# Stacked high and low parts for the last 64 rows of the feed-forward width in both down products

## The chip, the core and the metric

The kernel runs on one core of a Trainium2 chip. The metric is the device time of one execution in microseconds (us). The core has a matrix engine (TensorE; its weight loads have a row of their own in the profile, PEld), a vector engine (VectorE, DVE), a scalar engine (ScalarE, ACT), GpSimd (POOL), a queue that issues DMAs (SyncE, SP), and 16 DMA engines. The engines run side by side, each in its own order, and wait for each other through semaphores.

## The reference

One layer of an encoder on x of 1024 positions by 1024 channels, in float32, in three steps. The first and the last are feed-forwards of width 2752:

```python
def swiglu(x, w_gate, w_up, w_down):
    return (jax.nn.silu(x @ w_gate) * (x @ w_up)) @ w_down

h = layer_norm(ALPHA * h + 0.5 * swiglu(h, ffn1_w_gate, ffn1_w_up, ffn1_w_down), ln1_g, ln1_b)
h = layer_norm(ALPHA * h + hybrid_mixer(h, ...), ln2_g, ln2_b)
h = layer_norm(ALPHA * h + 0.5 * swiglu(h, ffn2_w_gate, ffn2_w_up, ffn2_w_down), ln3_g, ln3_b)
```

The mixer between them has one input projection, windowed attention with three strides, a Fourier branch, gates and an output projection. The change concerns the product with `w_down` in both feed-forwards, which contracts over the 2752 hidden channels.

## The kernel before

**Numbers.** A float32 operand is split into a high part (rounded to the format fp32r, in which TensorE takes float32 data in one pass) and a low part (what is left). A product is the sum of three matmuls, `TERMS` in line 331: high by high, high by low, low by high. `split` (line 340) makes the parts: `hi` copies on ScalarE (line 346), `lo` subtracts on VectorE (line 350); `pick` (line 337) chooses one.

**Products.** Each large product is a two by two block product done with seven block products instead of eight (`PROD`, line 380: product p multiplies one combination of the left blocks by one of the right blocks). The hidden width of 2752 is 21 blocks of 128 and a rest of 64. The blocks are taken in 11 pairs (`PAIRS`); a pair's even block belongs to the first half of the contraction and its odd block to the second. The odd block of the last pair, j = 10, is the rest of 64 rows, padded with zeros to 128: in `tail_after` (line 725) VectorE writes zeros to rows 64 to 127 of the hidden tile, and `_layouts` (line 2168) pads the weights with zero rows. The products that contract over odd blocks are 2 (a12 by b21), 3 (s4 by b22) and 4 (a22 by t4). Of their last pair, 64 rows of each operand or of one of them are zeros.

**The down product.** `ffn` (line 622) is called for tag "a" (the first feed-forward) and tag "b" (the second). Hidden tiles go to HBM (`spill`), and come back as steps: `load_step` (line 811) fetches, for product p and pair j, 512 columns of the left operand into the left half of a page and 512 columns of the right operand into the right half, two DMAs on SP's queue; `split` cuts the page into parts; `step` (line 819) issues 12 matmuls in line 827, three terms for each of four row tiles of 128, each 512 columns wide, into four PSUM banks. The order of the products is 1, 6, 2, 5, 3, 7, and in "a" then 4; their accumulators are X (products 1 and 2), Y (6), Z (5 and 3), V (7) and U (4). In "b" product 4 is done row tile by row tile: `load_b4` (line 856) keeps all right blocks in six pages (`qbb0` to `qbb5`), `load_a4` (line 863) fetches a strip of the left operand into two pages (`qab`, and `qsb` for pairs 8 to 10), and `last_steps` (line 844) issues 33 matmuls a row tile in line 852.

**The order of the work.** A planner, `Flow` (line 73), writes the program. TensorE's large jobs keep the order in which they are registered (`job`, with a cost in us: `MM` = 0.2267 a matmul); small ones are put between them when they are ready. Tasks of VectorE and ScalarE and loads are placed by the time at which the job that needs them is due, less a lead (34 us for the splits of the steps, 44 for their loads). The planner's clock goes by these costs alone; on the chip each engine then runs its list in order. So a change of a cost can shift the order of the lists.

**Names used below.** Tiles are named by their step: `qa210h` and `qa210l` are the parts of tag a, product 2, pair 10; `qb78l` is the low part of tag b, product 7, pair 8. Line 462 is the matmul of the gate, up and mixer input projections. Line 1600 is attention's product with the values, plain float32, which the trace shows as two records a matmul; where a window of keys is cut, it has pieces of 64 rows at rows 0 to 63 and 64 to 127. Line 1120 is a product of 32 rows by 387 columns, done once.

Of the kernel before, what the change touches and what calls it, by code (L numbers as in the profile page):

```python
# [10 lines left out]
F32 = mybir.dt.float32  # L11
F32R = mybir.dt.float32r
# [4 lines left out]
P = 128  # L17
# [2 lines left out]
KD = 8  # L20
FF = 2752
NFULL = FF // P
HEAD_DIM = 128
NH = 12
SLOTS = 4
# [16 lines left out]
PAIRS = 11  # L42
# [30 lines left out]
class Flow:  # L73
# [11 lines left out]
    def job(self, us, fn, banks=0, deps=(), **kw):  # L85
        self.jobs.append(Node("P", us, fn, deps, banks=banks, **kw))
        return self.jobs[-1]
# [82 lines left out]
    def short(self):  # L170

        return min((n.key for q in self.open.values() for n in q if not self.can(n) and self.shown(n)), default=1e9)
# [98 lines left out]
class Builder:  # L271
# [7 lines left out]
    def page(self, name, dt=F32):  # L279
        return self.sb.tile([P, 1024], dt, name=name, tag="pg", bufs=NPG)  # L280
# [15 lines left out]
def kernel(  # L296
# [6 lines left out]
    nc = tc.nc  # L303
    kb = Builder(ctx, tc)
    fl = Flow()
    page, half, bank = kb.page, kb.half, kb.bank
    V, S, G, Q, F, job = fl.V, fl.S, fl.G, fl.Q, fl.F, fl.job
    x, out = x[0], out[0]
# [22 lines left out]
    TERMS = (("hi", "hi"), ("hi", "lo"), ("lo", "hi"))  # L331
    MM = 0.2267
    stt = nc.vector.scalar_tensor_tensor
    L, R = slice(0, 512), slice(512, 1024)
    W, B, H, J = {}, {}, {}, {}

    def pick(parts, kind):
        return parts[0 if kind == "hi" else 1]

    def split(name, get, put, deps=(), need=None, lead=14.0, w=1024, pages=2, gives=1):  # L340

        st = {}

        def hi():
            st["h"] = page(name + "h", F32R)
            nc.scalar.activation(st["h"][:, :w], get()[:, :w], AF.Copy)

        def lo():
            t = page(name + "l", F32R)
            nc.vector.tensor_sub(t[:, :w], get()[:, :w], st["h"][:, :w].bitcast(F32))  # L350
            put((st["h"], t))
        us = 0.15 + w * 1.06e-3
        if isinstance(need, tuple):

            def piece(i):
                cs, last = slice(i * 512, (i + 1) * 512), None

                def hi_():
                    if i == 0:
                        st["h"] = page(name + "h", F32R)  # L360
                    nc.scalar.activation(st["h"][:, cs], get()[:, cs], AF.Copy)

                def lo_():
                    if i == 0:
                        st["l"] = page(name + "l", F32R)
                        put((st["h"], st["l"]))
                    nc.vector.tensor_sub(st["l"][:, cs], get()[:, cs], st["h"][:, cs].bitcast(F32))
                sn = S(0.6, hi_, deps[i], need[i], lead + 1.5, 1.3, pages=0 if i else 2)
                return V(0.69, lo_, [(sn, 0.1)], need[i], lead, gives=gives if i else 0)
            return [piece(0), piece(1)]  # L370
        s = S(0.15 + w * 0.88e-3, hi, deps, need, lead + 1.5, us + 0.6, pages=pages)
        return V(us, lo, [(s, 0.1)], need, lead, gives=gives)


# [97 lines left out]
    def put(c, names, parts):  # L472
        for i, n in enumerate(names):
            W[c, n] = tuple(t[:, i * 512:(i + 1) * 512] for t in parts)
# [147 lines left out]
    def ffn(tag, X, w_gu, w_tail, w_dn, load_rest, norm, rest_deps=None, sums_at=None, by_tile=False):  # L622

        HN = {}
        hs = {(n, j): kb.dram([P, 512], f"hs{tag}{n}{j}") for n in COMBOS for j in range(PAIRS)}
        PARTS = ((0, 4), (4, 8), (8, 11))
        TAIL = FF - NFULL * P
# [119 lines left out]
        c0 = ck[0]  # L747
        first = {"a11": J[c0, 1], "a12": J[c0, 2], "a21": None, "a22": J[c0, 4]}
# [14 lines left out]
        q = Q(J[tl, 0], 0.5, load_tail, pages=1)  # L763
# [20 lines left out]
        for si, (to, x0, x1) in enumerate(sums):  # L784
            for i in range(3):
# [7 lines left out]
                a = Q(at[0], 1.0, copy, [tdn[x0, i]] if x0 not in blk else [], lead=0.0)  # L793
# [3 lines left out]
        D_, Y, T, sm = {}, {}, {}, {}  # L797
# [4 lines left out]
        def source(n, j):  # L802
            if n in blk:
                return w_dn[blk[n], j]
            i = part_of(j)
            return td[n, i][j - PARTS[i][0]]

        def source_nodes(n, j):
            return [tdn[n, part_of(j)]] if n not in blk else []

        def load_step(p, j):
            def run():
                D_[p, j] = t = page(f"q{tag}{p}{j}")
                xn, wn = PROD[p]
                nc.sync.dma_start(t[:, L], hs[xn, j])
                nc.sync.dma_start(t[:, R], source(wn, j))
            return run

        def step(p, j, set_, first):
            def run():  # L820
                if first and j == 0:
                    for m in range(4):
                        B[tag, set_, m] = bank(f"{set_}{tag}{p}{m}")
                q = D_.pop((p, j))
                for m in range(4):
                    for ti, (a, b) in enumerate(TERMS):
                        nc.tensor.matmul(B[tag, set_, m], pick(q, a)[:, m * P:(m + 1) * P], pick(q, b)[:, R],  # L827
                                         start=first and j == 0 and ti == 0,
                                         stop=j == PAIRS - 1 and ti == 2, skip_group_check=True)
            return run  # L830

        if tag == "a":
# [3 lines left out]
        for p in (1, 6, 2, 5, 3, 7) if by_tile else (1, 6, 2, 5, 3, 7, 4):  # L836
            for j in range(PAIRS):
                first = p not in (2, 3)
                J[tag, "d", p, j] = n = job(12 * MM, step(p, j, SET[p], first), 4 if first and j == 0 else 0, gives=2)
                q = Q(n, 0.5, load_step(p, j), [(HN[PROD[p][0], j], 4.0)] + source_nodes(PROD[p][1], j), 44.0, pages=1)  # L840
                split(f"q{tag}{p}{j}", lambda p=p, j=j: D_[p, j], lambda t, p=p, j=j: D_.__setitem__((p, j), t), [q], n,
                      34.0)

        def last_steps(m, j0, j1):
            def run():
                if j0 == 0:
                    B[tag, "U", m] = bank(f"U{tag}{m}")
                for j in range(j0, j1):
                    aa, o = (D_["a", m], j) if j < 8 else (D_["as", m], j - 8)
                    bb, bs = D_["b", j // 2], slice((j % 2) * 512, (j % 2) * 512 + 512)  # L850
                    for ti, (a, b) in enumerate(TERMS):
                        nc.tensor.matmul(B[tag, "U", m], pick(aa, a)[:, o * P:(o + 1) * P], pick(bb, b)[:, bs],
                                         start=j == 0 and ti == 0, stop=j == PAIRS - 1 and ti == 2)
            return run

        def load_b4(i):
            def run():
                D_["b", i] = t = page(f"qb{tag}{i}")
                for j in range(2 * i, min(2 * i + 2, PAIRS)):
                    nc.sync.dma_start(t[:, (j % 2) * 512:(j % 2) * 512 + 512], source("t4", j))  # L860
            return run

        def load_a4(m):
            def run():
                D_["a", m], D_["as", m] = t, s = page(f"qa{tag}{m}"), page(f"qs{tag}{m}")
                for j in range(PAIRS):
                    dst = t[:, j * P:(j + 1) * P] if j < 8 else s[:, (j - 8) * P:(j - 7) * P]
                    nc.sync.dma_start(dst, hs["a22", j][:, m * P:(m + 1) * P])
            return run

        if by_tile:
            for m in range(4):
                for i, (j0, j1) in enumerate(PARTS):
                    J[tag, "u", m, i] = job(3 * (j1 - j0) * MM, last_steps(m, j0, j1), 1 if i == 0 else 0,
                                            gives=(4 if i == 2 else 0) + (12 if i == 2 and m == 3 else 0))

            for i in range((PAIRS + 1) // 2):
                n = J[tag, "u", 0, 0]
                deps = [x for j in range(2 * i, min(2 * i + 2, PAIRS)) for x in source_nodes("t4", j)]
                q = Q(n, 0.5, load_b4(i), deps, 88.0 - 8.0 * i, pages=1)  # L880
                split(f"qb{tag}{i}", lambda i=i: D_["b", i], lambda t, i=i: D_.__setitem__(("b", i), t), [q], n,
                      80.0 - 8.0 * i, 512 * min(2, PAIRS - 2 * i))
            for m in range(4):
                n = J[tag, "u", m, 0]
                q = Q(n, 0.75, load_a4(m), [(HN["a22", j], 4.0) for j in range(PAIRS)], pages=2)
                split(f"qa{tag}{m}", lambda m=m: D_["a", m], lambda t, m=m: D_.__setitem__(("a", m), t), [q], n)
                split(f"qs{tag}{m}", lambda m=m: D_["as", m], lambda t, m=m: D_.__setitem__(("as", m), t), [q], n, w=384)

        if rest_deps:
            rest_deps = rest_deps(ck)  # L890
# [334 lines left out]
    for p, bk, new in VORDER:  # L1225
        n = PROD[p][1]
        for i in range(2):
            value_part(n, i, (vblk if n in vblk else vt)[n][i], [vtn[n]] if n in vtn else (), VJ[p, 0], 14.0)
    for m in range(8):
        st = {}  # L1230
# [978 lines left out]
```

## Time and profile before

| | us |
|---|---|
| median of 3 runs | 2070.76 (2070.5 to 2072.65) |
| the profiled execution | 2072.24 |
| its span, first to last instruction | 2070.3 |
| TensorE matmul busy | 2058.5 (99%) |
| TensorE weight loads busy | 1713.6 (83%) |
| VectorE busy | 1276.4 (62%) |
| ScalarE busy | 910.4 (44%) |

The down products lie at 420 to 633 us (tag a) and 1853 to 2063 us (tag b) of the span. The page's busy times are of one profiled execution; matmuls are pipelined, so the start of a record tells more than its length, and the distance of two starts is the pace. In the rows, `128*128 128x512` is a matmul of 128 rows by 128 weight columns whose result is 128 by 512, and `64*128` one that contracts over 64 rows. SPq is SyncE's queue as it issues DMAs.

### The profile page before, as it was taken

How to read it: one execution, taken by the hardware profiler on the slowest of the kernel's cores; microseconds unless marked ns; L12 is line 12 of the kernel's file. 1: busy time of each engine (PE TensorE's matmuls, PEld its weight loads, DVE VectorE, ACT ScalarE, POOL GpSimd, SP SyncE). 2: the span in 40 equal slices, each digit the busy share in tenths (PEclk: the TensorE clock that was granted, in tenths of full speed). 3: DMA queues.
4: the chain of work that ended last, by engine and by line, in shares of the span. 5: the costliest groups of instructions: out<-in, count | busy, mean ns of one | idle time of the engine just before them, and what ended most of it. 6: DMA issues, size and time to landing. Idle time of an engine off the chain costs nothing.

```text
span 2070.3 us, 25541 instructions
## 1 busy us (share of the span) xinstructions
PE 2058.5 (99%) x9523; PEld 1713.6 (83%) x9523; DVE 1276.4 (62%) x1757; ACT 910.4 (44%) x1441; POOL 233.6 (11%) x404
## 2 busy tenths in 40 slices
PE   9999999999999999999999999999999999999998
PEld 7888888888888888888888888888888888888887
DVE  7865555576554658455556764763877665575565
ACT  6433333555475324455455443318633333355342
POOL 0122111010000010021121111000011101010000
PEclk9999999999999999999999999999999999999999
DMA  5778875599743336467786659523144433357743
GB/s 203 236 239 260 253 220 169 177 341 404 257 160 120 102 122 182 142 178 204 207 218 198 226 185 384 184 97 138 60 169 179 157 132 127 123 202 273 263 159 105
DMA packets 151292, 401.29 MB, mean 194 GB/s; under 512 B 18338, under 2 KB 40690, under 8 KB 150720
## 3 DMA queue, kind: packets, MB, share of 16 engines
q1 hardware_dynamic: 111648, 266.38, 37.2%
q0 software_dynamic: 39520, 133.28, 21.5%
q8 instruction: 74, 1.21, 0.2%
q14 instruction: 50, 0.41, 0.1%
HBM read 303.41 MB, written 153.84 MB: 221 GB/s over the span
## 4 chain that ended last, share of the span: by engine, by line
PE 97%; ACT 1%; DMA 1%; DVE 0%; issue 0%; DVEq 0%; SPq 0%
PE Ab L462 14%; PE Aa L462 13%; PE Aq L462 8%; PE Da L462 6%; PE Db L462 5%; PE As L462 5%; PE wo L2078 3%; PE Dq L462 3%; PE Zb L827 3%; PE Xb L827 3%; PE Za L827 3%; PE Xa L827 3%; PE pj L1991 2%; PE v L1238 2%; PE Ds L462 2%; PE pv L1600 2%
## 5 line engine op out<-in xcount | busy, mean ns | idle before, releaser
L1568 ACT ACTIVATE p<-p,stat 128x192 f32<-128x192 f32 (+2 forms) x96 | 42.3, 442 | 17.0 <-DVE stat L1563 16.0
L326 POOL DMA_DIRECT2D hsaa<-t2a x21 | 12.0, 571 | 317.1 <-DVE t2a L696 299.0
L1358 DVE SCALAR_TENSOR_TENSOR oq<-Dq,b_cols,t2q 128x512 f32<-128x512 f32 x12 | 11.8, 986 | 50.8 <-PE Dq L462 50.8
L326 POOL DMA_DIRECT2D hsba<-t2b x21 | 11.4, 543 | 279.6 <-DVE t2b L696 279.6
L1600 PEld LDWEIGHTS pv<-pT,v 128*128 128x128 f32 (+1 forms) x320 | 37.3, 189 | 6.1 <-ACT pT L1589 1.0
L692 DVE TENSOR_TENSOR t2b<-Db,t2b 128x512 f32<-128x512 f32 x21 | 14.5, 691 | 44.9 <-PE Db L462 44.9
L692 DVE TENSOR_TENSOR t2a<-Da,t2a 128x512 f32<-128x512 f32 x21 | 14.5, 691 | 44.4 <-PE Da L462 44.4
L600 ACT ACTIVATE t2a<-Aa 128x512 f32<-128x512 f32 x21 | 12.6, 600 | 65.5 <-PE Aa L462 65.4
L1600 PE MATMUL pv<-pT,v 128*128 128x128 f32 (+1 forms) x320 | 40.8, 289 | 0.5 <-ACT pT L1589 0.5
L600 ACT ACTIVATE t2b<-Ab 128x512 f32<-128x512 f32 x21 | 12.6, 599 | 62.9 <-PE Ab L462 62.9
L1553 DVE SCALAR_TENSOR_TENSOR p<-sc,bias 128x512 f32<-128x512 f32 (+1 forms) x40 | 24.7, 620 | 25.0 <-PE sc L1539 20.6
L326 POOL DMA_DIRECT2D n_spill<-y x16 | 8.6, 538 | 264.5 <-ACT y L1008 264.5
L1539 PE MATMUL sc<-oq,oq 128*128 128x192 f32 (+2 forms) x192 | 34.1, 322 | 0.0
L684 DVE TENSOR_TENSOR t3a<-Da,t3a 128x512 f32<-128x512 f32 x21 | 14.5, 690 | 27.8 <-PE Da L462 26.4
L1539 PEld LDWEIGHTS sc<-oq,oq 128*128 128x128 f32 x192 | 29.8, 190 | 2.0
L1358 DVE SCALAR_TENSOR_TENSOR oq<-Dq,b_cols,t3q 128x512 f32<-128x512 f32 x12 | 11.8, 987 | 30.1 <-PE Dq L462 30.1
L462 PE MATMUL Db<-Zs40h,usb 128*128 128x512 f32 x84 | 29.4, 391 | 0.7 <-DVE t3b L684 0.7
L462 PE MATMUL Db<-Zs41h,usb 128*128 128x512 f32 x84 | 29.3, 389 | 0.0
L462 PE MATMUL Da<-Xs40h,usa 128*128 128x512 f32 x84 | 29.3, 389 | 0.0
L462 PE MATMUL Da<-Xs41h,usa 128*128 128x512 f32 x84 | 29.3, 389 | 0.0
L684 DVE TENSOR_TENSOR t3b<-Db,t3b 128x512 f32<-128x512 f32 x21 | 14.5, 690 | 20.7 <-PE Db L462 16.0
L1563 DVE TENSOR_REDUCE stat<-p 128x2 f32<-128x384 f32 (+2 forms) x40 | 24.5, 620 | 1.2
(7340 smaller groups left out, 7210.4 us busy)
## 6 DMA issues: line engine op xcount, KB each, us to landing
qa<-hsas SPq DMA_DIRECT2D x44, 256.0 KB, 5.9
qa<-tdat SPq DMA_DIRECT2D x44, 256.0 KB, 5.4
qb<-hsbs SPq DMA_DIRECT2D x44, 256.0 KB, 4.4
ga<-in_ffn_gu_dram SPq DMA_DIRECT2D x21, 512.0 KB, 6.1
ua<-in_ffn_gu_dram SPq DMA_DIRECT2D x21, 512.0 KB, 8.4
gb<-in_ffn_gu_dram SPq DMA_DIRECT2D x21, 512.0 KB, 3.5
ub<-in_ffn_gu_dram SPq DMA_DIRECT2D x21, 512.0 KB, 4.4
qa<-hsaa SPq DMA_DIRECT2D x33, 256.0 KB, 4.8
```

The costliest lines, as they stand in the source:

```text
L326: nc.gpsimd.dma_start(*a, **kw)
L462: nc.tensor.matmul(out, pick(w, a)[:, k * P:(k + 1) * P], self.cols(xn, b, k), start=first and k == 0 and ti == 0, stop=last and k == 3 an ...
L600: nc.scalar.activation(H[c, t], B[c, "B"], AF.Copy)
L684: nc.vector.tensor_sub(H[c, "t3"], B[c, "D"], H[c, "t3"])
L692: nc.vector.tensor_sub(H[c, "t2"], B.pop((c, "D")), H[c, "t2"])
L827: nc.tensor.matmul(B[tag, set_, m], pick(q, a)[:, m * P:(m + 1) * P], pick(q, b)[:, R], start=first and j == 0 and ti == 0, stop=j == PAIR ...
L1238: nc.tensor.matmul(ps, X2.cols(f"a{hf + 1}{k // 4 + 1}", a, k % 4)[:, mm * P:(mm + 1) * P], pick(wv, b), start=(k == 0 and ti == 0), stop= ...
L1539: nc.tensor.matmul(sv[:, i, :], qk[0][:, qt * P:(qt + 1) * P], qk[1][:, k0:k0 + w], start=True, stop=True, skip_group_check=True)
L1568: nc.scalar.activation(p3()[:, i, :], p3()[:, i, :], AF.Exp, bias=stats[h][:, k, 0:1], scale=1.0, accum_out=stats[h][:, k, 1:2])
L1600: nc.tensor.matmul(out_of(tiles.index(qt)), env["v"][kc, rows], pt[r0:r0 + rows, sl * P:(sl + 1) * P], start=qt not in seen, stop=last, sk ...
L1991: nc.tensor.matmul(bk[hf], pick(wv, a)[:, k, cc * P:(cc + 1) * P], pick(attn[k], b)[:, hf * 512:(hf + 1) * 512], start=(k == 0 and ti == 0 ...
L2078: nc.tensor.matmul(bk[i], pick(merged[k], a)[:, ms], pick(wo[k], b)[:, i * 512:(i + 1) * 512], start=(k == 4 * gi and ti == 0), stop=(k == ...
```

## The change

For pair 10 of products 2, 3 and 4 (`short`) the operands' 64 rows are loaded twice, into rows 0 to 63 and into rows 64 to 127 (`both`, two DMAs of half the size instead of one). The high part is made of the whole tile as before. The remainder of the left operand is written into the lower half of its own high tile, so that this tile holds the high part in rows 0 to 63 and the low part in rows 64 to 127; the right operand's tile holds its high part in both halves. The remainder of the right operand goes to rows 0 to 63 of the low tile. `split` gets `under`, the column range of the left operand, and makes these pieces with up to two subtractions on VectorE. One matmul over 128 rows then gives high by high plus low by high, and a second one over 64 rows gives high by low (`terms`, with `few`). So these steps issue 8 matmuls instead of 12; in "b", product 4 issues 32 a row tile instead of 33. The planner's costs of these jobs follow.

```diff
@@ -20,6 +20,7 @@
 KD = 8
 FF = 2752
 NFULL = FF // P
+TAIL = FF - NFULL * P
 HEAD_DIM = 128
 NH = 12
 SLOTS = 4
@@ -337,7 +338,7 @@
     def pick(parts, kind):
         return parts[0 if kind == "hi" else 1]
 
-    def split(name, get, put, deps=(), need=None, lead=14.0, w=1024, pages=2, gives=1):
+    def split(name, get, put, deps=(), need=None, lead=14.0, w=1024, pages=2, gives=1, under=None):
 
         st = {}
 
@@ -346,9 +347,19 @@
             nc.scalar.activation(st["h"][:, :w], get()[:, :w], AF.Copy)
 
         def lo():
-            t = page(name + "l", F32R)
-            nc.vector.tensor_sub(t[:, :w], get()[:, :w], st["h"][:, :w].bitcast(F32))
-            put((st["h"], t))
+            t, h = page(name + "l", F32R), st["h"]
+            if under is None:
+                nc.vector.tensor_sub(t[:, :w], get()[:, :w], h[:, :w].bitcast(F32))
+            else:
+
+                c0, c1 = under
+                if c0 > 0:
+                    nc.vector.tensor_sub(t[:, :c0], get()[:, :c0], h[:, :c0].bitcast(F32))
+                if c1 > c0:
+                    nc.vector.tensor_sub(h[TAIL:, c0:c1], get()[TAIL:, c0:c1], h[TAIL:, c0:c1].bitcast(F32))
+                if c1 < w:
+                    nc.vector.tensor_sub(t[:TAIL, c1:w], get()[:TAIL, c1:w], h[:TAIL, c1:w].bitcast(F32))
+            put((h, t))
         us = 0.15 + w * 1.06e-3
         if isinstance(need, tuple):
 
@@ -808,12 +819,33 @@
         def source_nodes(n, j):
             return [tdn[n, part_of(j)]] if n not in blk else []
 
+        def both(dst, src, j):
+
+            if j is None:
+                nc.sync.dma_start(dst, src)
+            else:
+                nc.sync.dma_start(dst[:TAIL], src[:TAIL])
+                nc.sync.dma_start(dst[TAIL:], src[:TAIL])
+
+        def short(p, j):
+            return p in (2, 3, 4) and j == PAIRS - 1
+
+        def terms(bank_, x, w, xs, ws, first, last, few):
+
+            if few:
+                todo = ((x[0][:, xs], w[0][:, ws]), (x[0][:TAIL, xs], w[1][:TAIL, ws]))
+            else:
+                todo = [(pick(x, a)[:, xs], pick(w, b)[:, ws]) for a, b in TERMS]
+            for ti, (a, b) in enumerate(todo):
+                nc.tensor.matmul(bank_, a, b, start=first and ti == 0, stop=last and ti == len(todo) - 1,
+                                 skip_group_check=True)
+
         def load_step(p, j):
             def run():
                 D_[p, j] = t = page(f"q{tag}{p}{j}")
                 xn, wn = PROD[p]
-                nc.sync.dma_start(t[:, L], hs[xn, j])
-                nc.sync.dma_start(t[:, R], source(wn, j))
+                both(t[:, L], hs[xn, j], j if short(p, j) else None)
+                both(t[:, R], source(wn, j), j if short(p, j) else None)
             return run
 
         def step(p, j, set_, first):
@@ -823,10 +855,8 @@
                         B[tag, set_, m] = bank(f"{set_}{tag}{p}{m}")
                 q = D_.pop((p, j))
                 for m in range(4):
-                    for ti, (a, b) in enumerate(TERMS):
-                        nc.tensor.matmul(B[tag, set_, m], pick(q, a)[:, m * P:(m + 1) * P], pick(q, b)[:, R],
-                                         start=first and j == 0 and ti == 0,
-                                         stop=j == PAIRS - 1 and ti == 2, skip_group_check=True)
+                    terms(B[tag, set_, m], q, q, slice(m * P, (m + 1) * P), R, first and j == 0, j == PAIRS - 1,
+                          short(p, j))
             return run
 
         if tag == "a":
@@ -836,10 +866,10 @@
         for p in (1, 6, 2, 5, 3, 7) if by_tile else (1, 6, 2, 5, 3, 7, 4):
             for j in range(PAIRS):
                 first = p not in (2, 3)
-                J[tag, "d", p, j] = n = job(12 * MM, step(p, j, SET[p], first), 4 if first and j == 0 else 0, gives=2)
+                J[tag, "d", p, j] = n = job((8 if short(p, j) else 12) * MM, step(p, j, SET[p], first), 4 if first and j == 0 else 0, gives=2)
                 q = Q(n, 0.5, load_step(p, j), [(HN[PROD[p][0], j], 4.0)] + source_nodes(PROD[p][1], j), 44.0, pages=1)
                 split(f"q{tag}{p}{j}", lambda p=p, j=j: D_[p, j], lambda t, p=p, j=j: D_.__setitem__((p, j), t), [q], n,
-                      34.0)
+                      34.0, under=(0, 512) if short(p, j) else None)
 
         def last_steps(m, j0, j1):
             def run():
@@ -848,16 +878,14 @@
                 for j in range(j0, j1):
                     aa, o = (D_["a", m], j) if j < 8 else (D_["as", m], j - 8)
                     bb, bs = D_["b", j // 2], slice((j % 2) * 512, (j % 2) * 512 + 512)
-                    for ti, (a, b) in enumerate(TERMS):
-                        nc.tensor.matmul(B[tag, "U", m], pick(aa, a)[:, o * P:(o + 1) * P], pick(bb, b)[:, bs],
-                                         start=j == 0 and ti == 0, stop=j == PAIRS - 1 and ti == 2)
+                    terms(B[tag, "U", m], aa, bb, slice(o * P, (o + 1) * P), bs, j == 0, j == PAIRS - 1, short(4, j))
             return run
 
         def load_b4(i):
             def run():
                 D_["b", i] = t = page(f"qb{tag}{i}")
                 for j in range(2 * i, min(2 * i + 2, PAIRS)):
-                    nc.sync.dma_start(t[:, (j % 2) * 512:(j % 2) * 512 + 512], source("t4", j))
+                    both(t[:, (j % 2) * 512:(j % 2) * 512 + 512], source("t4", j), j if short(4, j) else None)
             return run
 
         def load_a4(m):
@@ -865,13 +893,13 @@
                 D_["a", m], D_["as", m] = t, s = page(f"qa{tag}{m}"), page(f"qs{tag}{m}")
                 for j in range(PAIRS):
                     dst = t[:, j * P:(j + 1) * P] if j < 8 else s[:, (j - 8) * P:(j - 7) * P]
-                    nc.sync.dma_start(dst, hs["a22", j][:, m * P:(m + 1) * P])
+                    both(dst, hs["a22", j][:, m * P:(m + 1) * P], j if short(4, j) else None)
             return run
 
         if by_tile:
             for m in range(4):
                 for i, (j0, j1) in enumerate(PARTS):
-                    J[tag, "u", m, i] = job(3 * (j1 - j0) * MM, last_steps(m, j0, j1), 1 if i == 0 else 0,
+                    J[tag, "u", m, i] = job((3 * (j1 - j0) - int(i == 2)) * MM, last_steps(m, j0, j1), 1 if i == 0 else 0,
                                             gives=(4 if i == 2 else 0) + (12 if i == 2 and m == 3 else 0))
 
             for i in range((PAIRS + 1) // 2):
@@ -879,12 +907,13 @@
                 deps = [x for j in range(2 * i, min(2 * i + 2, PAIRS)) for x in source_nodes("t4", j)]
                 q = Q(n, 0.5, load_b4(i), deps, 88.0 - 8.0 * i, pages=1)
                 split(f"qb{tag}{i}", lambda i=i: D_["b", i], lambda t, i=i: D_.__setitem__(("b", i), t), [q], n,
-                      80.0 - 8.0 * i, 512 * min(2, PAIRS - 2 * i))
+                      80.0 - 8.0 * i, 512 * min(2, PAIRS - 2 * i), under=(0, 0) if short(4, 2 * i) else None)
             for m in range(4):
                 n = J[tag, "u", m, 0]
                 q = Q(n, 0.75, load_a4(m), [(HN["a22", j], 4.0) for j in range(PAIRS)], pages=2)
                 split(f"qa{tag}{m}", lambda m=m: D_["a", m], lambda t, m=m: D_.__setitem__(("a", m), t), [q], n)
-                split(f"qs{tag}{m}", lambda m=m: D_["as", m], lambda t, m=m: D_.__setitem__(("as", m), t), [q], n, w=384)
+                split(f"qs{tag}{m}", lambda m=m: D_["as", m], lambda t, m=m: D_.__setitem__(("as", m), t), [q], n, w=384,
+                      under=(256, 384))
 
         if rest_deps:
             rest_deps = rest_deps(ck)
```

## Rows read from the trace of the kernel before

**Rows 1.** The page: busy us by engine, TensorE clock by slice
```profile
PE 2058.5 (99%) x9523; PEld 1713.6 (83%) x9523; DVE 1276.4 (62%) x1757; ACT 910.4 (44%) x1441; POOL 233.6 (11%) x404
...
PEclk9999999999999999999999999999999999999999
```

**Rows 2.** Chain of waits, both down products: start us, us, what
```profile
420.25 29.92 PE Xa L827 x132
...
2033.03 29.93 PE Ub L852 x132
...
2062.98 0.71 DVE yb L942 x2
```

**Rows 3.** TensorE waits, first and last of seven: total us, times, longest
```profile
PE warm L2116 <- DVE eps L322: 1.4, 1, 1.4
...
PE Aa L462 <- DVE Xa110l L367: 0.2, 1, 0.2
```

**Rows 4.** Both down stages: us; busy PE, PEld, DVE, ACT, POOL; clock; DMA
```profile
420.09:633.15 213.06, 213.06 (x958) 176.92 (x957) 129.63 (x158) 108.61 (x134) 15.97 (x30) 1.00 0.78 275
1853.34:2062.79 209.45, 209.45 (x925) 173.24 (x923) 125.29 (x154) 81.01 (x93) 3.75 (x7) 1.00 0.60 208
```

**Rows 5.** Attention: a group of 833.79 to 835.64, then timeline (start, us)
```profile
L1600 PE MATMUL pv<-pT,v 64*128 64x128 f32 x4 | 0.5, 322 | 0.0
...
833.79 1.92 PE L1600 MATMUL pv<-pT,v 128*128 128x128 f32 x16
...
835.98 0.40 PE L462 MATMUL Aq<-Ya220l,t34q3h 128*128 128x512 f32 x1
```

**Rows 6.** Timeline of TensorE, a block of full height alone, from 960.41
```profile
960.41 1.05 PE L1600 MATMUL pv<-pT,v 128*128 128x128 f32 x8
961.30 0.60 PE L1584 MATMUL pt<-ident,p 128*128 128x128 f32 x4
...
961.97 0.40 PE L462 MATMUL Dq<-Ys10l,t12q8h 128*128 128x512 f32 x1
```

**Rows 7.** Timeline of weight loads (PEld) around the 64-row matmuls of rows 5
```profile
834.80 0.30 PEld L1600 LDWEIGHTS pv<-pT,v 128*128 128x128 f32 x2
...
835.22 0.19 PEld L1600 LDWEIGHTS pv<-pT,v 64*128 64x128 f32 x2
...
835.33 0.19 PEld L1600 LDWEIGHTS pv<-pT,v 64*128 64x128 f32 x2
835.64 0.19 PEld L462 LDWEIGHTS Aq<-Ya220h,t34q3h 128*128 128x128 f32 x1
835.75 0.19 PEld L462 LDWEIGHTS Aq<-Ya220l,t34q3h 128*128 128x128 f32 x1
```

**Rows 8.** Timeline of TensorE after the two 32-row matmuls of line 1120
```profile
144.49 0.81 PE L1120 MATMUL ln_ps<-oh,rb 32*12 32x387 f32 x2
145.23 0.50 PE L462 MATMUL Aa<-Xs20h,t12a7h 128*128 128x512 f32 x1
145.57 0.39 PE L462 MATMUL Aa<-Xs20l,t12a7h 128*128 128x512 f32 x1
```

**Rows 9.** Lines and tiles: ns min/median/max, first and last start us
```profile
L827 PEld LDWEIGHTS Xa<-qa210l,qa210h x4: 187/188/188, 507.1 to 509.2; 128*128 128x128 f32 x4
...
L350 DVE TENSOR_TENSOR qa210l<-qa,qa210h x1: 1224/1224/1224, 490.2 to 490.2; 128x1024 fp32r<-128x1024 f32 x1
...
L350 DVE TENSOR_TENSOR qbb5l<-qbb,qbb5h x1: 683/683/683, 2018.3 to 2018.3; 128x512 fp32r<-128x512 f32 x1
...
L815 SPq DMA_DIRECT2D qa<-hsas x44: 319/320/1331, 409.2 to 546.5; - x44
...
L868 SPq DMA_DIRECT2D qab<-hsba x32: 376/430/1182, 2012.6 to 2034.9; - x32
...
L827 PE MATMUL Vb<-qb78l,qb78h x4: 389/389/389, 2024.9 to 2027.0; 128*128 128x512 f32 x4
...
L350 DVE TENSOR_TENSOR qb78l<-qb,qb78h x1: 1218/1218/1218, 2014.9 to 2014.9; 128x1024 fp32r<-128x1024 f32 x1
```

## The prediction

> **What bounds the kernel now.** I read the busy shares first [rows 1]. [...] A modelled busy time is no proof, so the chain of waits comes next [rows 2]: both down products lie on it whole, product after product with nothing between. One product is 132 matmuls in 29.92 us, 0.2267 us each, and the end follows directly from the last one: 2062.98 is the first VectorE piece after it. The list of TensorE's own waits has seven rows, from 1.4 us (the warm-up at the start) down to 0.2 us, about 4.3 us in all [rows 3]; none lies in the two stages that the change touches, where TensorE is busy for the whole of both stretches and VectorE for 60% [rows 4]. So TensorE's instruction stream is the bound, and anything that shortens or lengthens it there moves the end one for one. Loads, VectorE and the queues matter only if they become late.
>
> **What is removed.** Block step j = 10 of products 2, 3 and 4 takes two matmuls for each of four row tiles instead of three. That is three products in each of two feed-forwards: 3 x 4 x 2 = 24 matmuls gone, 24 x 0.2267 = **5.44 us** [rows 2]. All of it is on the path that sets the end.
>
> **What is added on TensorE.** The two matmuls that remain differ in height: the first contracts over 128 rows (high and low parts stacked), the second over 64 rows. Their order is 128, 64, 128, 64, so TensorE goes into a 64-row matmul 24 times and out of it 24 times; the last one ends the kernel's matmuls, so 47 changes of height count. Does a change cost anything? The kernel before has 64-row matmuls in attention, line 1600, so the trace can tell. There, 12 records of full height and 4 of 64 rows stand ahead of an input-projection matmul; from the first record to the second projection matmul it is 835.98 - 833.79 = 2.19 us [rows 5]. A reference block of 12 full records ahead of the same kind of matmul takes 961.97 - 960.41 = 1.56 us [rows 6]. The four 64-row records account for 0.63 us. They run in pairs (both halves of the array at once: the weight loads come as x2 at 835.22 and x2 at 835.33), so their streams are worth 2 x 0.11 = 0.22 us. The other 0.41 us belongs to two changes of height, 0.20 us each.
>
> The weight loads show what it is [rows 7]. Full-height loads follow each other in about 0.11 us, each one under the matmul before it (0.30 us for two that last 0.19). The first 64-row load comes at 835.22, 0.31 us after the load that began at 834.91 (834.80 + 0.11), so it wasn't pulled under the running matmul; and its matmul can't stream before the load is done, 0.11 us later (835.33). Going back is alike: the full-height load at 835.64 stands 0.31 us behind 835.33, and the next one follows after 0.11. So at each change TensorE lets the running matmul leave the array, then loads weights in the open. A third place has a wider stream: after two 32-row matmuls of 387 columns, starting 0.32 us apart (the pair's 0.81 us less the 0.49 us that one record lasts), the second projection matmul comes at 145.57, 0.76 us after the start at 144.81 [rows 8]; less the 0.32 of its own stream and 0.23 of the first projection matmul, 0.21 us are left. The price doesn't shrink when the stream is longer.
>
> For the 512-wide matmuls of this change I take **0.195 us a change**. The upper end of the direct readings is 0.205. [...] Further out, the least would be the weight load alone in the open, 0.11 us [rows 7], and the most a wait for the whole recorded matmul and then the load: 0.39 + 0.11 - 0.23 = 0.27 us (0.39 is what a projection matmul's record lasts when nothing delays it, as at 145.57 [rows 8]). A gain below nothing is excluded: a 64-row matmul streams its columns no faster than a full one (0.11 us for 128 columns in both), and nothing here runs beside it in the other half. 47 x 0.195 = **9.17 us** added; a short step then takes 8 x 0.2267 + 8 x 0.195 = 3.37 us where 2.72 stood.
>
> The trace shows a gap of 0.20 us at each change of height, in both directions [rows 7]. [...]
>
> **What is added elsewhere.** Remainders: a 1024-wide subtraction takes 1.224 us and a 512-wide one 0.683, so one split in two costs 0.14 us more; five short steps and four strips of the last product make 9 x 0.14 = 1.3 us of VectorE, spread over stages where it idles 40% [rows 4, 9]. Loads: 15 more issues on SP's queue (two a step in five steps, one for the last block of t4, one in each of four strips), 0.32 to 0.43 us each, 5 to 6 us over 420 us; the bytes stay the same [rows 9]. The new wait: the first matmul of a short step now needs VectorE's remainder, as before it needed ScalarE's copy; behind it waits TensorE's whole stream, since it keeps its order. What covers all three is the distance from a remainder to its first use. The smallest in the down products is 8.8 us (ends at 2014.9 + 1.2, first needed at 2024.9) [rows 9], and j = 10 of products 2 and 3 has more: that of product 2 in the first feed-forward ends at 491.5 and is used from 507.1 on [rows 9]. A step that loses 0.5 us of it stays covered, so I cost these at nothing; without cover the loss would be about 0.5 us a step, 3 us in all.
>
> The planner books a short step at 8 x 0.2267 = 1.81 us, while the sum says 3.37, so its clock runs up to 1.56 us a step ahead of TensorE's: loads and remainders come a little early in the order, within the same cover. Its lists may come out in another order around the change. Before, waits were so small [rows 3] that this can hardly give anything back; I allow 0 to 2 us of loss.
>
> **The sum.** -5.44 + 9.17 = +3.73 us, 0.18%. The profiled execution took 2072.24 us, its span of 2070.3 and 1.9 around it; it stands 1.5 us above the median of the runs, 2070.76, to which I apply the difference: **2074.5 us**. A measurement of this kernel can tell about 0.2% from no change, 4.1 us, so the forecast lies just inside it.
>
> **Rivals.**
> (a) Changes of height are free here, because the 64-row matmul of this number format is run as a full one with empty rows. For it: a 64-row matmul alone needs no second half. Against it: the 32-row pair of rows 8 has no partner in the array either, and paid. Then 2070.76 - 5.44 = 2065.3 us, faster.
> (b) Only the weight load is exposed, 0.11 us: 47 x 0.11 - 5.44 = -0.3, 2070.5 us, no change. Against it: the loads that came 0.20 us late.
> (c) The drain is dearer behind a 512-wide stream, up to the whole record: 0.27 us, 47 x 0.27 - 5.44 = +7.3, 2078.1 us, slower. It decides from (5.44 + 4.14) / 47 = 0.204 us a change, a hair above what I take. For it: 0.205 and 0.21 are among the readings, and no row shows it behind this width. Against it: from 128 to 387 columns it moved by 0.01 us at most.
> (d) The price is as forecast, and the new order of the lists makes TensorE wait 1 to 2 us more somewhere: 2075.5 to 2076.5, slower.
>
> **How the numbers follow.** Forecast 0.43, (a) 0.08, (b) 0.07, (c) 0.27, (d) 0.15. Faster is (a), 0.08. Within 0.2% are the forecast and (b), 0.50. Slower are (c) and (d), 0.42. The range runs from 2071.5, leaving out (a) and (b), to the end of (c), 2078.1. The likeliest case's own range, with 0.187 to 0.204 a change, is 2074.1 to 2074.9.
>
> **What would show it.** Each short step should last about 3.4 us where 2.72 us stood, products 2, 3 and 4 about 30.6 us instead of 29.92; a 128-row matmul and the 64-row one after it should start 0.42 us apart, with the 64-row load beginning some 0.3 us after the matmul before it. Products 1, 5, 6 and 7 keep 29.92 us. If a short step takes 1.81 us, (a) holds and my central step is wrong; about 2.7 us, (b); over 3.45 us, (c). New waits in TensorE's list would show (d), or loads that lost their cover.

## The result, and the profile after

The changed kernel takes 2076.41 us, the kernel before 2071.76 us (medians of 13 runs each): a ratio of 1.0021, 95% interval [1.0014, 1.0029], or 4.65 us slower, between 2.9 and 6.0. The forecast was 3.73 us slower; the range held the time. Its 2074.5 us stood on the 2070.76 us of three earlier runs of the kernel before, which took 1.0 us more beside the change. The point lies just beyond the bound of 0.2%, and the interval reaches across it.

The page's first part and TensorE's waits in the changed kernel:

```profile
PE 2063.4 (99%) x9499; PEld 1708.2 (82%) x9499; DVE 1278.5 (62%) x1766; ACT 911.2 (44%) x1441; POOL 233.5 (11%) x404
...
PE warm L2145 <- DVE eps L323: 1.4, 1, 1.4
...
PE Db L473 <- DVE t3b L695: 0.2, 1, 0.2
```

Beside [rows 1]: 24 matmuls fewer (9499 against 9523), and TensorE busy for 4.9 us more. Its list of waits (engine, line, what it waited for; us in total, times, longest) is as short as in [rows 3]. So the time did not go into waits: the stream of matmuls itself became longer.

The chain of waits through the down products (start us, us, tile, line, count), beside [rows 2]:

```profile
420.34 29.92 PE Xa L840 x132
450.26 29.92 PE Ya L840 x132
480.18 30.41 PE Xa L840 x128
510.59 60.53 PE Za L840 x260
571.13 11.08 PE Va L840 x48
...
604.78 30.41 PE Ua L840 x128
635.20 11.09 PE v L1267 x48
...
1855.15 29.92 PE Xb L840 x132
...
2036.06 30.43 PE Ub L840 x128
...
2066.51 0.71 DVE yb L971 x2
```

The same chain in the kernel before, where [rows 2] leaves it out, and one of its waits that [rows 3] leaves out:

```profile
569.85 10.88 PE Va L827 x48
...
633.23 10.89 PE v L1238 x48
...
1853.51 29.92 PE Xb L827 x132
...
PE Db L462 <- DVE t3b L684: 0.7, 1, 0.7
```

Products 1 and 6 (the first Xa and Ya) keep their 29.92 us. Products 2, 3 and 4 have four matmuls fewer and take longer: 30.41 us, and 0.20 us more that falls into the first matmul of whatever follows (11.08 and 11.09 us, where 48 full matmuls take 10.88 and 10.89). The first down product grew from 212.98 us (420.25 to 633.23) to 214.86 + 0.20, by 2.08 us; the second from 209.47 (1853.51 to 2062.98) to 211.36, by 1.89. Together that is 3.97 us of the 4.0 us by which the span grew (2074.3 against 2070.3). The rest cancels: one wait on the way to the second product was 0.5 us shorter (0.2 here, 0.7 us in the profiled execution of before), and the end, from the first VectorE piece behind the last matmul to the end of the span, was 0.5 us longer.

One short step on TensorE, and the weight loads under it, both as a timeline (start us, us, engine, line, out<-in, shape):

```profile
507.22 0.39 PE L840 MATMUL Xa<-qa210h 128*128 128x512 f32 x1
507.53 0.50 PE L840 MATMUL Xa<-qa210l,qa210h 64*128 64x512 f32 x1
507.96 0.49 PE L840 MATMUL Xa<-qa210h 128*128 128x512 f32 x1
508.39 0.50 PE L840 MATMUL Xa<-qa210l,qa210h 64*128 64x512 f32 x1
...
507.53 0.18 PEld L840 LDWEIGHTS Xa<-qa210l,qa210h 64*128 64x128 f32 x1 [0.35 <-issue]
507.96 0.19 PEld L840 LDWEIGHTS Xa<-qa210h 128*128 128x128 f32 x1 [0.24 <-issue]
508.39 0.18 PEld L840 LDWEIGHTS Xa<-qa210l,qa210h 64*128 64x128 f32 x1 [0.24 <-issue]
```

It is the picture of [rows 7] again, now 512 columns wide. Matmuls start 0.43 us apart where 0.227 is the pace. A load no longer starts with the matmul before it: the first 64-row load begins 0.31 us behind the start of the full matmul at 507.22, and PEld stands still for 0.24 to 0.35 us before each.

### The profile page after: what moved, and what is told of

It reads as the page before. It is cut to its first block, busy times and chain, and to the rows that moved or that the text cites. A ratio compares the mean times of both kernels' runs of the same rounds, so it can differ in the third digit from the quotient of the medians.

```text
span 2074.3 us, 25535 instructions
## 1 busy us (share of the span) xinstructions
PE 2063.4 (99%) x9499; PEld 1708.2 (82%) x9499; DVE 1278.5 (62%) x1766; ACT 911.2 (44%) x1441; POOL 233.5 (11%) x404
## 4 chain that ended last, share of the span: by engine, by line
PE 97%; ACT 1%; DMA 1%; DVE 0%; issue 0%; SPq 0%; DVEq 0%; ACTq 0%
PE Aa L473 14%; PE Ab L473 13%; PE Aq L473 8%; PE Da L473 6%; PE Db L473 5%; PE As L473 5%; PE wo L2107 3%; PE Dq L473 3%; PE Zb L840 3%; PE Za L840 3%; PE Xb L840 3%; PE Xa L840 3%; PE v L1267 2%; PE pj L2020 2%; PE Ds L473 2%; PE pv L1629 2%
```

## Experiments

By the forecast each change between a 128-row and a 64-row matmul costs TensorE a fixed time. Two other theories were to be told apart from it: that the 64-row matmul is itself slow, wherever it stands, and that the loss comes from the side work (loads, remainders, the planner's order). Every kernel ran beside the kernel before; a difference is against those runs, and the bracket behind a ratio is its 95% interval.

**e1, grouped.** The four 128-row matmuls of a short step first, then the four of 64 rows:

```diff
+                if short(p, j):
+                    for m in range(4):
+                        nc.tensor.matmul(B[tag, set_, m], q[0][:, m * P:(m + 1) * P], q[0][:, R], ...)
+                    for m in range(4):
+                        nc.tensor.matmul(B[tag, set_, m], q[0][:TAIL, m * P:(m + 1) * P], q[1][:TAIL, R], ...)
+                    return
```

> The changed kernel, but in the five short steps the four matmuls of 128 rows come first and the four of 64 rows after them; loads, remainders and planner costs are as in the change. TensorE then changes height twice a step instead of eight times, 5 x 2 + 7 = 17 times in all (the last product of the second feed-forward keeps its order). If each change of height costs 0.20 us: 17 x 0.20 - 5.44 = -2.0 us against the kernel before, and a short step of about 2.2 us. If it is the 64-row matmul itself that is slow (0.40 us more each time it runs, whatever stands beside it), the order doesn't matter: about +4 us as in the change.

Measured: 2070.61 us against 2071.74, ratio 0.9996 [0.9988, 1.0005], 1.1 us less. The same eight matmuls, only in another order, are 5.8 us faster than in the change (1.1 less against 4.65 more). So it isn't the 64-row matmul as such. Timeline of a short step:

```profile
506.67 1.07 PE L859 MATMUL Xa<-qa210h 128*128 128x512 f32 x4
507.66 1.20 PE L862 MATMUL Xa<-qa210l,qa210h 64*128 64x512 f32 x4
508.79 0.50 PE L840 MATMUL Za<-qa50h 128*128 128x512 f32 x1
509.13 0.40 PE L840 MATMUL Za<-qa50l,qa50h 128*128 128x512 f32 x1
```

From 506.67 to 509.13 nine matmuls start in 2.46 us, where nine full paces are 2.04: 0.42 us more, for two changes of height. The gain is 0.9 us smaller than expected; the table below says where that went.

**e2, full height.** The second matmul runs over 128 rows too; the lower halves add low by low:

```diff
-                todo = ((x[0][:, xs], w[0][:, ws]), (x[0][:TAIL, xs], w[1][:TAIL, ws]))
+                todo = ((x[0][:, xs], w[0][:, ws]), (x[0][:, xs], w[1][:, ws]))
...
-                    nc.vector.tensor_sub(t[:TAIL, c1:w], get()[:TAIL, c1:w], h[:TAIL, c1:w].bitcast(F32))
+                    nc.vector.tensor_sub(t[:, c1:w], get()[:, c1:w], h[:, c1:w].bitcast(F32))
```

> The changed kernel, but the second matmul of a short step runs over 128 rows too: the right operand's remainder is made over all 128 rows, so the matmul also adds the product of the two low parts. No change of height is left, the 24 matmuls stay removed, and the doubled loads, the split remainders and the planner costs stay. If the changes of height are the whole loss: -5.44 us against the kernel before, a short step of 1.81 us. If the extra loads, the split remainders or the planner's new order cost something, it is nearer to the kernel before, by that much.

Measured: 2067.79 against 2071.74 us, ratio 0.9980 [0.9972, 0.9989], 3.95 us less: faster than the kernel before and than the change. Chain of waits, the short products of "a", the way to the end of "b":

```profile
479.79 29.01 PE Xa L840 x128
508.81 58.93 PE Za L840 x260
...
1850.20 29.92 PE Xb L840 x132
...
2056.95 0.71 DVE yb L971 x2
```

Four matmuls fewer are now 0.91 us less (29.01), and the second product takes 206.75 us, 2.72 = 12 x 0.2267 less than before. All of the 5.44 us arrives in the two products; 1.5 us are lost behind the last matmul, which e5 and e6 look into.

**e3, the price alone.** The kernel before, with low by high of the pairs concerned over 64 rows:

```diff
+                        rs = slice(0, TAIL if p in (2, 3, 4) and j == PAIRS - 1 and ti == 2 else P)
-                        nc.tensor.matmul(B[tag, set_, m], pick(q, a)[:, m * P:(m + 1) * P], pick(q, b)[:, R],
+                        nc.tensor.matmul(B[tag, set_, m], pick(q, a)[rs, m * P:(m + 1) * P], pick(q, b)[rs, R],
```

(and the same in line 852 for tag b).

> The kernel before with all its matmuls, loads, remainders and planner costs; only the third of the three matmuls (low by high) of the pairs concerned runs over the upper 64 rows. 47 changes of height, nothing removed. If a change costs 0.20 us: +9.4 us against the kernel before, 3.4 + 0.9 = 4.3 us a step where 2.72 stood. If the loss in the change came from loads, remainders or the order of the lists: about 0.

Measured: 2081.21 against 2071.74 us, ratio 1.0047 [1.0034, 1.0060], 9.5 us more with 9.4 expected. No load, no remainder and no planner cost differ from the kernel before, and no matmul is gone, so the changes of height alone make these 9.5 us. Chain of waits:

```profile
480.07 31.32 PE Xa L828 x132
...
1857.51 29.92 PE Xb L828 x132
...
2071.59 0.71 DVE yb L944 x2
```

The second product takes 214.08 us, 4.61 more than before, for 23 changes: 0.200 us each.

**e4, all three over 64 rows.** As e3, with the slice for every term:

```diff
+                        rs = slice(0, TAIL if p in (2, 3, 4) and j == PAIRS - 1 else P)
```

> The kernel before, but all three matmuls of the pairs concerned run over 64 rows: 72 matmuls of 64 rows, 5 x 2 + 7 = 17 changes of height, nothing removed. If only the change of height costs: 17 x 0.20 = +3.4 us against the kernel before, and within a step the matmuls start 0.227 us apart as ever. If a 64-row matmul is itself slower by 0.40 us: 72 x 0.40 = +29 us. If it streams in half the time: -72 x 0.11 + 3.4 = -4.5 us.

Measured: 2075.92 against 2071.74 us, ratio 1.0021 [1.0012, 1.0030], 4.2 us more. Timeline of TensorE:

```profile
507.18 0.39 PE L828 MATMUL Xa<-qa29h,qa29l 128*128 128x512 f32 x1
507.50 0.49 PE L828 MATMUL Xa<-qa210h 64*128 64x512 f32 x1
507.84 0.39 PE L828 MATMUL Xa<-qa210l,qa210h 64*128 64x512 f32 x1
508.07 0.39 PE L828 MATMUL Xa<-qa210h,qa210l 64*128 64x512 f32 x1
...
510.15 0.39 PE L828 MATMUL Xa<-qa210h,qa210l 64*128 64x512 f32 x1
510.46 0.50 PE L828 MATMUL Za<-qa50h 128*128 128x512 f32 x1
```

Within the run of 64-row matmuls the pace is (510.15 - 507.84) / 10 = 0.231 us: not slower by 0.4, not half as long either. Gaps stand at the two ends alone. The 0.004 us above 0.227 are a small second cost, found in e1 too: for some matmuls behind a change the starts are 0.23 to 0.24 us apart.

**e8, in pairs.** The short step as 128, 64, 64, 128, 128, 64, 64, 128:

```diff
+                        two = (slice(0, P), 0), (slice(0, TAIL), 1)
+                        for i, (rs, part) in enumerate(two if m % 2 == 0 else two[::-1]):
+                            nc.tensor.matmul(B[tag, set_, m], q[0][rs, m * P:(m + 1) * P], q[part][rs, R], ...)
```

> The changed kernel, but in the five short steps the heights run 128, 64, 64, 128, 128, 64, 64, 128: four changes of height a step instead of eight, 5 x 4 + 7 = 27 in all. If the loss goes with the number of changes at 0.20 us each: 27 x 0.20 - 5.44 = 0.0 us against the kernel before, between the change (47 changes) and the grouped order (17). If it goes with the number of 64-row matmuls: +4 us as in the change.

Measured: 2071.92 against 2071.68 us, ratio 1.0002 [0.9993, 1.0011]. 47, 27, 17 and 0 changes give +4.65, +0.2, -1.1 and -3.95 us.

**e7, the planner's costs alone.** The kernel before with 8 instead of 12 matmuls booked for a short step:

```diff
-                ... job(12 * MM, step(p, j, SET[p], first), ...)
+                ... job((8 if p in (2, 3, 4) and j == PAIRS - 1 else 12) * MM, step(p, j, SET[p], first), ...)
```

> The kernel before with the planner's new costs alone (8 instead of 12 matmuls booked for a short step), all instructions as before. If the new order of the lists costs nothing, the time of the kernel before, 0 +- 0.5 us in the spans; if the lists come out worse, TensorE waits 1 to 2 us more somewhere.

Measured: 2071.89 against 2071.68 us, ratio 1.0004 [0.9995, 1.0013]. The second product takes as long as before to 0.01 us. The wait of 0.7 us for t3b, gone here, is also gone in e3, whose planner costs are those of before, and stands in e4, which has them too, with 0.7 us; so it doesn't go with the planner's costs.

**e6, the side work alone.** The kernel before, with the 15 loads concerned cut into two DMAs of 64 rows and the nine remainders cut in two:

```diff
-                nc.sync.dma_start(t[:, L], hs[xn, j])
-                nc.sync.dma_start(t[:, R], source(wn, j))
+                for cs, src in ((L, hs[xn, j]), (R, source(wn, j))):
+                    if p in (2, 3, 4) and j == PAIRS - 1:
+                        nc.sync.dma_start(t[:64, cs], src[:64])
+                        nc.sync.dma_start(t[64:, cs], src[64:])
+                    else:
+                        nc.sync.dma_start(t[:, cs], src)
...
+            for c0, c1 in (((0, cut), (cut, w)) if cut else ((0, w),)):
+                nc.vector.tensor_sub(t[:, c0:c1], get()[:, c0:c1], st["h"][:, c0:c1].bitcast(F32))
```

> The kernel before with the change's side work alone: the 15 further DMA issues (the same loads cut in two halves of 64 rows) and the nine remainders cut in two, all matmuls and planner costs as before. If the side work is covered as the prediction says: within 0.5 us of the kernel before in both down products, plus what an instruction fetch at the end may add, 0.4 to 0.9 us. If it isn't: TensorE shows waits in the short steps, up to 0.5 us each, 3 us in all.

Measured: 2073.42 against 2071.68 us, ratio 1.0009 [1.0000, 1.0019], 1.7 us more; the interval begins at no difference. The chain of waits shows where it isn't:

```profile
1853.12 29.92 PE Xb L832 x132
...
2062.60 0.71 DVE yb L957 x2
```

The second product takes 209.48 us, as before, and TensorE gained no wait in either. The time is at the end: from that VectorE piece to the end of the span it is 8.8 us (2062.60 to 2071.4) where the kernel before has 7.3 (2062.98 to 2070.3), 1.5 more where 0.4 to 0.9 was expected. Traffic by queue in the last stretch, 2067 to 2071.4 us:

```profile
q1 hardware_dynamic: 287, 0.52, 31.8%
q14 instruction: 2, 0.02, 1.1%
```

Two packets of instruction fetch come behind the last store; the last stretch of before has none.

**e5, one load.** The kernel of e2, with a doubled load as one DMA whose source repeats the 64 rows:

```diff
-                nc.sync.dma_start(dst[:TAIL], src[:TAIL])
-                nc.sync.dma_start(dst[TAIL:], src[:TAIL])
+                two = bass.AP(tensor=src.tensor, offset=src.offset,
+                              ap=[[0, 2], [src.ap[0][0], TAIL], list(src.ap[1])])
+                nc.sync.dma_start(dst, two)
```

> The kernel of e2 (both matmuls over 128 rows), with each doubled load issued as one DMA whose source repeats the 64 rows, so SP's queue issues as many DMAs as the kernel before. In e2 the stretch from the last matmul to the end was 1.5 us longer than before, with an instruction fetch behind the last store. If the 15 added issues caused that: the stretch is back near 7.7 us, and the whole gain of 5.4 us arrives (a span near 2064.9). If the nine added subtractions or chance caused it: a span as in e2, 2065.8, with the fetch still behind the last store.

Measured: 2083.01 against 2071.68 us, ratio 1.0053 [1.0040, 1.0067], 11.3 us more, which no theory expected. Waits in 460 to 590 us, then the chain of waits, then the DMA share and GB/s in 40 slices of 1900 to 1904 us:

```profile
PE Za L841 <- DVE ya L953: 13.6, 1, 13.6
ACT qa210h L347 <- DMA qa<-in_ffn_down_dram: 12.5, 1, 12.5
...
ACT qa310h L347 <- DMA qa<-in_ffn_down_dram: 9.7, 1, 9.7
DVE qa310h L359 <- ACT qa310h L347: 9.6, 1, 9.6
...
533.86 14.76 DMA qa<-in_ffn_down_dram
553.10 32.14 PE Za L841 x128
...
DMA  9343332211111111111111111111111111139993
GB/s 307 143 144 123 123 143 82 102 62 41 61 41 61 41 41 61 41 61 41 61 41 61 41 41 61 41 61 41 61 41 41 61 41 61 41 143 184 246 184 61
```

While such a load is under way, 41 to 61 GB/s move at a share of a tenth of the 16 DMA engines, what one or two of them would be; before and behind it the rate is some two to six times that. What in such a source sets this rate, no run shows.

The load for `qa310` (product 3) took 14.76 us from issue to landing. ScalarE's copy of it waited, and VectorE, which keeps its order, stood 9.6 us for that copy. Behind it in VectorE's list comes line 953, which reads the accumulators of product 5, and for that TensorE waited 13.6 us before product 3. In the page's clock row the slice of 520.6 to 572.7 us, in which this wait lies, is the only one of 40 below the top tenth (8 in place of 9), and the 128 matmuls behind the wait took 32.14 us instead of e2's 29.01. The cover that the prediction counted, from a remainder to its first use, did not run out: `qa210` was ready at 500.9 and used from 507.3, `qa310` ready at 551.2 and used from 583.3. The late load held up what stands behind its copy and its remainders in the engines' lists, here line 953, and by it TensorE.

For its question e5 still answers: the nine subtractions are in it and the 15 issues are not, and the end is 7.4 us (2075.04 to 2082.4), as before.

**The sums.** For each kernel: how the two products differ from before (chain of waits, the last change of the first product included; e1's from its timeline), how the end differs, and what was measured.

| kernel | changes of height | first product | second product | end | sum | measured |
|---|---|---|---|---|---|---|
| the change | 47 | +2.08 | +1.89 | +0.5 | +4.5 | +4.65 |
| e1 | 17 | -1.37 | -0.37 | +0.5 | -1.2 | -1.1 |
| e2 | 0 | -2.72 | -2.72 | +1.5 | -3.9 | -3.95 |
| e3 | 47 | +4.80 | +4.61 | 0 | +9.4 | +9.5 |
| e4 | 17 | +1.41 | +2.46 | 0 | +3.9 | +4.2 |
| e5 | 0 | +14.05 | -2.72 | 0 | +11.3 | +11.3 |
| e6 | 0 | 0 | +0.01 | +1.5 | +1.5 | +1.7 |
| e7 | 0 | 0 | +0.01 | 0 | 0 | +0.2 |
| e8 | 27 | -0.12 | +0.42 | +0.5 | +0.8 | +0.2 |

In e1, e4 and e8 the products are 0.1 to 0.3 us longer than 0.20 us a change gives, the slightly slower pace behind a change into a run of one height. In e5 the first product holds the wait of 13.6 us and 3.1 us more in the 128 matmuls behind it. For e1, e6, e7 and e8 the interval of the ratio takes in no difference or begins at it; what carries the argument there is the length of the products, which agrees with before to 0.01 us where nothing in them was changed (e6, e7).

The end is 0.5 or 1.5 us longer in every kernel with the 15 further issues on SP's queue and in none without them; e6 has the issues and e5 has the subtractions without them, so it goes with the issues. Instruction fetch over the whole execution (queue, kind: packets, MB, share), in before, in the change and in e6:

```profile
q14 instruction: 50, 0.41, 0.1%
...
q14 instruction: 51, 0.42, 0.1%
...
q14 instruction: 52, 0.43, 0.1%
```

All kernels fall in line: 50 packets where the end is as before (before, e3, e4, e5, e7), 51 where it is 0.5 us longer (the change, e1, e8), 52 where it is 1.5 us longer (e2, e6), and the further ones lie in the last stretch. That the fetch causes the delay is not shown, since no run took the packets away alone, and there is one profiled execution of each kernel. Why the same 15 issues bring one packet here and two there stays open.

## Why the prediction was right

**The bound.** TensorE's stream set the time before and sets it after: the sums above, made from TensorE and the end alone, meet the measured differences within 0.6 us.

**What is removed** measured as said: e2 shows 2.72 us less in each product, 5.44 us in all.

**The price of a change of height** was the central step, read from attention's 64-row matmuls in [rows 5] to [rows 7] and from the 32-row pair in [rows 8], none of them of this format or width. Taken: 0.195 us, with 0.187 to 0.205. No run shows 0.187, the author's estimate for the lower end, or 0.195, which was taken between it and 0.205; the readings were 0.20 to 0.21, and e3 measured 0.200. 47 changes are 9.4 us where the sum had 9.17. With it the two products should be 47 x 0.200 - 5.44 = 3.96 us longer, and they are 3.97 us longer. The signs that were named stood in the trace: starts 0.43 us apart, the first 64-row load 0.31 us behind the matmul before it, products 2 to 4 longer by some 0.7 us, the others unchanged. That TensorE lets the running matmul leave the array and then loads weights in the open is the author's inference from these load starts; no run took the two apart.

**The side work** in the two products cost nothing, as said (e6), and the planner's new costs too (e7); 0 to 2 us had been allowed. The term that was missed is the end: the queue was costed by its issue time and its cover alone, and 15 more issues made the way from the last matmul to the end 0.5 us longer in the change, 1.5 in e2 and e6. It is a tenth of the result here and more than a quarter of the 5.44 us in e2. The cover was right for these loads, but it was not the whole condition, as e5 shows: its late load of `qa310` cost TensorE a wait of 13.6 us through VectorE's order, 30 us before the load's own step was due.

**The rivals.** (a) and (b) fall with e3: a change isn't free, nor does it cost the load's 0.11 us alone, but 0.200. (c) would have had to come from more than 0.204 us a change; it is 0.200, the same behind 512 columns as it was read behind 128. (d), new waits, didn't appear in the change. That the forecast lies at the bound between no change and slower was said. Of the 0.92 us by which the measured difference exceeds it, 0.23 come from the price (9.4 instead of 9.17) and 0.5 from the end; the rest is within the interval of 2.9 to 6.0, so on which side of the bound the kernel falls is not settled by these runs.

## What to carry to other kernels

Where TensorE is the bound, count the changes between matmul heights, not only the matmuls: here each change cost 0.20 us, so that saving one matmul of 0.227 us while adding two changes was a loss. Filling the short matmul up to full height with something harmless (here the product of the low parts, from rows that were loaded anyway) kept the gain in the products (e2, 2.72 us in each); where that can't be done, group matmuls of one height (e1, whose 1.1 us less is not clear of no difference). And look for the price of a new form in whatever the old kernel already does in that form, even in another stage.

## What was not expected

A DMA whose source begins with a dimension of 2 that repeats its rows moved some 50 GB/s at a tenth of the DMA engines' share, where ScalarE waited 9.7 us for the load of `qa310`, against 1.0 us for the two DMAs of half the size in e2; such loads in a dense stretch held TensorE for 13.6 us (e5), by way of VectorE's list. And 15 further DMA issues, hidden everywhere else, went with a longer end, by 0.5 us with one further packet of instruction fetch and by 1.5 with two (e6, e2, the change).
